# A two-layer streaming encoder on one core: masked attention over its decays, a fifth key tile, one inverse buffer, a split last norm, another seed

## The chip, the cores and the metric

The kernel runs on one core of one Trainium2 chip. The metric is the device time of one execution in microseconds, as the median over runs. The core has five engines that run side by side, each in the order in which its instructions are written: PE (matrix products, with its weight loads shown as PEld), DVE (vector work), ACT (scalar functions and copies), POOL (small vector work) and SP, which in this kernel issues all the DMAs. Semaphores hold an instruction back until what it reads is there.

## The reference

The input is x (2048 frames of 1024 values) with a conditioning vector c. There are two layers, each `x = x + gate * Mixer(RMSNorm(x) * (1 + scale) + shift)`, and a last RMSNorm. The first mixer is an RG-LRU block, the second a gated delta rule with 8 heads of width 128, in chunks of 64 in the reference:

```python
a_mat = where(strict, einsum(k_beta, k) * decay_mask, 0)
t_mat = triangular_solve(a_mat + eye, eye)
attn  = where(causal, einsum(q, k) * decay_mask, 0)
# step over the chunks:
v_new = u_c - w_c @ state
o_c   = q_c @ state + attn_c @ v_new
state = state * e_c + k_c.T @ v_new
...
y = rmsnorm(x, final_g)
```

All values are fp32.

## The kernel before

Frames are taken in two halves of 1024 (`u`), each in two pieces of 512 (`i`), each piece in four blocks of 128 (`b`). The projections are 512-wide products in which each fp32 factor is split in a high and a low part, three products for one (`products`, line 711). A weight panel of 1024x128 is loaded (`raw`), cast to its high part on ACT (`whi`) and, the first time, its low part is made on DVE (`wlo`).

In the second layer each head `h`, half `u` and piece `i` has threads of its own. `key_thread` loads the summed log decays as a row to all partitions (tile `ec`), masks them on POOL, takes the exponential on ACT, transposes the keys on PE (`pk`), copies them to `kd`, and multiplies the products of keys (`pkk`) by the decays to `ac`. `norm_q_thread` squares the queries reloaded in token order (`pq`), `value_thread` scales the values (`vn`). `query_thread` multiplies the products of keys and queries (`pqk`) by the decays to the masked attention `at` and then gives the decay tile back. `inverses_thread` inverts blocks of 32 on DVE, and `levels_thread` joins them to blocks of 128 with small products (`px`, `pr`) through the buffer `tf`. `recurrence_thread` then steps over the blocks: on PE `pp` (keys and queries with the state), on DVE `zt`, on PE `py`, on ACT `yt`, on PE `pS`, on DVE the new state. Each step waits for the one before, and projection products (`mm`) of later heads fill PE meanwhile. `t2` is ACT's scaled copy of the queries' product.

ACT holds one table of functions at a time: the exponential and the tanh need another than the silu that makes `kt`, `qt`, `vt` and the gate `tz`, and each change is an `ACT_TABLE_LOAD`.

The order on every engine is set before the kernel runs, by a planner (`Weave`): threads yield what they want next (an engine with a duration, a buffer, an event), and it always takes the one that can start first. The durations off PE are scattered by 1% with a random number from `SEED`, so another seed gives another order everywhere. Buffers are counted by `Slots`, a number for each tag: 3 for `ec`, 4 for `atn`, 4 for `kd`, 2 for `tf`. Tags in the pool `l2a` lie in a stretch of memory that is given back early, by `queries_end_thread`, to the rows and residuals of the last stage.

In the last stage (`out2_jobs`, products `mmo`) `final_thread` adds the residual and sums squares of each part of a block, and `finish_thread` normalizes it. The last block has three parts (512, 256, 256 columns).

Of the kernel before, what the change touches and what calls it, by code (L numbers as in the profile page):

```python
# [16 lines left out]
D = 1024  # L17
# [8 lines left out]
NH = 8  # L26
# [4 lines left out]
TURN = 2  # L31
BLK = 2
KTN, QTN = 6, 5
MARGIN = 1.0
EPS = 1e-6
SMALL = 161
# [1 line left out]

LAG = {"pe": 0.2, "act": 0.128, "dve": 0.113, "pool": 0.034}
WEIGHTS = 0.12  # L40
SEED, SPREAD = 3, 0.01
TABLE = 1.28
TRANSFER = {"sp": (1.56, 0.61, 0.05), "st": (0.74, 0.38, 0.5)}
SHARED = {"dve2": "pool2", "pool2": "dve2"}
# [126 lines left out]
def trunk_kernel(ctx, tc, x, head, small, ada0, ada_w, ada_b, final_g, w1, gate_w, ow1, w2, wab, ow2, out):  # L171
# [44 lines left out]
    def part_of(tile_in, at, *shape):  # L216
# [24 lines left out]
    tags |= {"edge1": ("l1", 1)}  # L241
    tags |= {"yf": ("o1", 1), "yh": ("o1", 2), "yl": ("o1", 2), "xr": ("o1", 2), "g1": ("o1", 1)}
    tags |= {t: ("l2", n) for t, n in {
        "xe": 2, "xf": 2, "kt": KTN, "qt": QTN, "vt": 1, "ec": 3, "gr": 1, "middle": 1, "ac": 4, "atn": 4, "kd": 4, "vn": 4,
        "rq": 4, "nk": 4, "oo": 2, "tblk": 1, "ttmp": 1, "tf": 2, "zt": 2, "t2": 2, "yt": 2, "so": 2, "ro": 2,
        "ssk": 2, "ssq": 2, "rk": 2, "cc": 2, "junk": 1, "ab": 1, "gin": 1, "gg": 1, "spe": 1, "spd": 1, "beta": 2,
        "gs": 2, "eg": 2}.items()}

    for t in ("xe", "xf", "vt", "ec", "gr", "middle", "ab", "gin", "gg", "spe", "spd"):
        tags[t] = ("l2a", tags[t][1])  # L250
    tags |= {"g2": ("o2a", 1), "fg": ("o2a", 1), "xta": ("o2a", 2)}
    tags |= {"oh": ("o2", 3), "ol": ("o2", 3), "xt": ("o2", 4), "ot": ("o2", 2)}
    slots = {t: Slots(n) for t, (_, n) in tags.items()}
    slots["turn"] = Slots(TURN)
    pools.update(xp=xp, ps=ps)
    phase, early = ExitStack(), ExitStack()

# [14 lines left out]
    def ev(*key):  # L272
        return events.setdefault(key, Event())

    def put(tag, token):
        w.put(slots[tag], token)
# [848 lines left out]
    def key_thread(u, h, i):  # L1125
# [2 lines left out]
        g_d = yield ev("grows", u)  # L1128
        etok = yield slots["ec"]
        yield "sp", 0.92  # L1130
        ec = tile_([P, TB, P], "ec", "ec")
        sp.dma_start(out=ec, in_=g_d[h:h + 1, i * TC:(i + 1) * TC].to_broadcast([P, TC]))
        yield "none", MARGIN / 2
        yield "pool", 0.779, MARGIN / 2
# [126 lines left out]
    def query_thread(u, h, i):  # L1261
        qt, qtok = yield ev("q", u, h, i)
        kt, ktok, ac, atok, ec, etok, kd, dtok = (yield ev("key", u, h, i))[:-2]
        ptok = yield slots["tp"]
        pqk = ps.tile([P, TB, P], F32, tag="tp", name="pqk")
        for b in range(TB):
            yield "pe", 0.224, 0.0
            pe.matmul(pqk[:, b, :], lhsT=kt[:, b * P:(b + 1) * P], rhs=qt[:, b * P:(b + 1) * P],  # L1268
                      start=True, stop=True)
        xtok = yield slots["atn"]  # L1270
        yield "dve", 0.61
        at = tile_([P, TB, P], "atn", "at")
        dve.tensor_tensor(at, pqk, ec, ALU.mult)
        put("tp", ptok)
        put("ec", etok)
        vn, ntk = yield ev("vn", u, h, i)
        toks = {"kt": ktok, "qt": qtok, "ac": atok, "atn": xtok, "kd": dtok, "vn": ntk}
        w.set(ev("parts", u, h, i), (kt, qt, ac, at, kd, vn, toks))

    def inverses_thread(u, h):  # L1280

# [114 lines left out]
    def recurrence_thread(u, h):  # L1396
# [4 lines left out]
        for i in range(NTC):  # L1401
# [7 lines left out]
            for b in range(TB):  # L1409
                m = i * TB + b  # L1410

                first, last = u + m == 0, u == NU - 1 and m == NB - 1
                kc, qc = kt[:, b * P:(b + 1) * P], qt[:, b * P:(b + 1) * P]
                if first:
                    pp = hold = None
                    zt = vn[:, b, :]
                else:
                    ptok = yield slots["d"]
                    yield "pe", 0.442
                    pp = ps.tile([P, 2, P], F32, tag="d", name="pp")  # L1420
                    pe.matmul(pp[:, 0, :], lhsT=kc, rhs=S_, start=True, stop=True)  # L1421
                    pe.matmul(pp[:, 1, :], lhsT=qc, rhs=S_, start=True, stop=True)  # L1422
                    hold = Hold(w, slots["d"], ptok, 2)
                if b == TB - 1:
                    release(toks, "kt", "qt")
                if not first:
                    ztok = yield slots["zt"]
                    yield "dve", 0.265
                    zt = tile_([P, P], "zt", "zt")
                    dve.scalar_tensor_tensor(zt, pp[:, 0, :], eg[:, 0, m, h:h + 1], vn[:, b, :], ALU.mult,  # L1430
                                             ALU.subtract)
                    hold.done()

                w.spawn(output_thread(u, h, m, pp, hold, oo[:, b, :], so[:, b:b + 1], eg), 1)
                ptok = yield slots["d"]
                yield "pe", 0.216
                py = ps.tile([P, P], F32, tag="d", name="py")
                pe.matmul(py, lhsT=rm[:, b, :], rhs=zt, start=True, stop=True)  # L1438
                if not first:
                    put("zt", ztok)  # L1440
                ytok = yield slots["yt"]
                yield "act", 0.18
                yt = tile_([P, P], "yt", "yt")
                act.activation(yt, py, AF.Copy, scale=1.0 if first else -1.0)
                put("d", ptok)
                ptok = yield slots["d"]
                yield "pe", M4 if last else 2 * M4
                pS = ps.tile([P, 2, P], F32, tag="d", name="pS")
                if not last:
                    pe.matmul(pS[:, 0, :], lhsT=kd[:, b, :], rhs=yt, start=True, stop=True)  # L1450
                pe.matmul(pS[:, 1, :], lhsT=at[:, b, :], rhs=yt, start=True, stop=True)  # L1451
                put("yt", ytok)
                hold = Hold(w, slots["d"], ptok, 1 if last else 2)
                w.set(ev("pS", u, h, m), (pS, hold))
                if b == TB - 1:
                    release(toks, "ac", "vn", "kd", "atn")
                if last:
                    return
                yield "dve", 0.258
                if first:  # L1460
                    dve.tensor_copy(out=S_, in_=pS[:, 0, :])
                else:
                    dve.scalar_tensor_tensor(S_, S_, eg[:, 1, m, h:h + 1], pS[:, 0, :], ALU.mult, ALU.add)
                hold.done()
# [73 lines left out]
    def queries_end_thread():  # L1538
        for i in range(NTC):
            yield ev("parts", NU - 1, NH - 1, i)  # L1540
            yield ev("rq", NU - 1, NH - 1, i)
        early.close()
        enter("o2a")
        w.set(ev("o2a"))
# [94 lines left out]
    def finish_thread(b, parts):  # L1639
        xt, tag, tok = yield ev("xt", b)  # L1640
        otag = "raw" if b < AHEAD else "ot"
        otok = yield slots[otag]
        stok = yield slots["ss"]
        ot = tile_([P, D], otag, "ot")
# [4 lines left out]
        if parts > 2:  # L1649
            yield "dve", 0.605  # L1650
            dve.tensor_tensor(xt[:, 0:TC], xt[:, 0:TC], fg[:, 0:TC], ALU.mult)
        for q in range(1, parts):
            yield ev("sq", b, q)
            yield "pool", 0.309
            pool.tensor_tensor(ss[:, 0:1], ss[:, 0:1], ss[:, q:q + 1], ALU.add)
        rtok = yield slots["rs"]
        yield "pool", 1.34
        rs = tile_([P, 1], "rs", "rs")
        rsqrt(rs, ss[:, 0:1], 1.0 / D, 1)
        put("ss", stok)  # L1660
        if parts > 2:
            yield "act", 0.628
# [133 lines left out]
```

## Time and profile before

| what | value |
|---|---|
| median of 3 runs | 1860.39 us (1857.08 to 1862.02) |
| the profiled execution, its own time | 1852.99 us |
| its span, first to last instruction | 1851.3 us |
| PE busy | 1798.8 us |
| ACT busy | 1167.0 us |
| granted clock, mean | 0.996 |

The span is what lies between the first and last instruction of one execution, and the time of that execution is 1.7 us more. A busy PE is a union of modelled intervals, so short gaps between products that overlap don't show in it. In the groups a line's idle time is that just ahead of its instructions, with what ended it.

### The profile page before, as it was taken

What the parts mean: (1) busy time and instruction counts of PE and PEld (TensorE: products, weight loads), DVE (VectorE), ACT (ScalarE), POOL (GpSimd) and SP (SyncE); (2) the same over time, 40 slices, a digit from 0 to 9 for tenths busy, and PEclk for the clock granted to TensorE, in tenths of its full rate; (3) what the DMA queues carried; (4) which work ended last, traced back from release to release, by engine and by line L of the source; (5) the groups of instructions that cost most, each with busy time, mean ns of one, the idle gap of its engine ahead of it and who ended that gap; (6) DMA issues with size and microseconds to landing.
All of it is one profiled execution on the core that took longest, in us unless ns stands there. A gap on an engine that the chain in (4) does not pass through costs nothing.

```text
span 1851.3 us, 31018 instructions
## 1 busy us (share of the span) xinstructions
PE 1798.8 (97%) x10270; PEld 1441.3 (78%) x10270; DVE 1344.0 (73%) x3112; ACT 1167.0 (63%) x2709; POOL 358.4 (19%) x896
## 2 busy tenths in 40 slices
PE   6999999999999999999999999999999999999998
PEld 4777777777878877787888787787788877778886
DVE  7989887877455647777888878577776687776653
ACT  5766777666111467786888766777778678654221
POOL 2111001010000013232323221232223223211100
PEclk9999999999999999999999999999999999999999
DMA  9577655545588645567677666366655556687741
GB/s 357 146 205 210 238 190 179 184 156 165 191 217 222 188 126 141 142 167 182 165 165 195 155 162 191 106 162 151 150 141 138 145 142 162 151 224 208 245 144 67
DMA packets 510425, 322.75 MB, mean 174 GB/s; under 512 B 369844, under 2 KB 437940, under 8 KB 510264
## 3 DMA queue, kind: packets, MB, share of 16 engines
q1 hardware_dynamic: 510264, 320.77, 62.0%
q8 instruction: 81, 1.33, 0.3%
q14 instruction: 80, 0.66, 0.1%
HBM read 219.93 MB, written 100.73 MB: 173 GB/s over the span
## 4 chain that ended last, share of the span: by engine, by line
PE 71%; DVE 9%; DMA 7%; ACT 7%; SPq 4%; issue 2%; POOL 1%; DVEq 0%; POOLq 0%; ACTq 0%
PE mm L711 39%; PE mmo L711 18%; PE pg L843 3%; DVE xf L763 2%; DMA raw<-in_w 2%; PE py L1438 1%; PE pp L1421 1%; PE pS L1450 1%; PE pS L1451 1%; PE pp L1422 1%; DVE ttmp L1303 1%; DVE tblk L1306 1%; DMA blk<-blk_d 1%; PE pqk L1268 1%; PE pkk L1180 1%
## 5 line engine op out<-in xcount | busy, mean ns | idle before, releaser
L763 DVE SCALAR_TENSOR_TENSOR xf<-xe,small_s,xf 128x512 f32<-128x512 f32 x288 | 214.1, 749 | 40.8 <-ACT xf L1021 37.2
L687 ACT CAST whi<-raw 128x1024 fp32r<-128x1024 f32 x96 | 100.0, 1042 | 50.1 <-DMA raw<-in_w 43.7
L1303 DVE TENSOR_TENSOR ttmp<-blk,tblk 128x60 f32<-128x60 f32 (+24 forms) x496 | 105.5, 213 | 17.3 <-DMA blk<-blk_d 5.7
L1306 DVE TENSOR_TENSOR tblk<-tblk,ttmp 128x60 f32<-128x60 f32 (+24 forms) x496 | 107.4, 217 | 12.2
L711 PE MATMUL mm<-hh_('in2', 0)_5148,whi 128*128 128x512 f32 x256 | 103.9, 406 | 2.2 <-DVE tf L1350 2.2
L711 PE MATMUL mm<-hh_('in2', 1)_11583,whi 128*128 128x512 f32 x256 | 104.5, 408 | 0.7 <-ACT tz L1036 0.7
L711 PE MATMUL mm<-hh_('in2', 0)_5148,wlo 128*128 128x512 f32 x256 | 104.2, 407 | 0.0
L711 PE MATMUL mm<-hh_('in2', 1)_11803,wlo 128*128 128x512 f32 x256 | 104.1, 407 | 0.0
L711 PE MATMUL mm<-hl_('in2', 1)_11584,whi 128*128 128x512 f32 x256 | 104.0, 406 | 0.0
L711 PE MATMUL mm<-hh_('in2', 1)_11583,wlo 128*128 128x512 f32 x256 | 104.0, 406 | 0.0
L711 PE MATMUL mm<-hl_('in2', 0)_5149,whi 128*128 128x512 f32 x256 | 103.8, 406 | 0.0
L711 PE MATMUL mm<-hl_('in2', 0)_5034,whi 128*128 128x512 f32 x256 | 103.6, 405 | 0.0
L711 PE MATMUL mm<-hl_('in2', 1)_11804,whi 128*128 128x512 f32 x256 | 103.5, 404 | 0.0
L711 PE MATMUL mm<-hh_('in2', 1)_11803,whi 128*128 128x512 f32 x256 | 103.5, 404 | 0.0
L711 PE MATMUL mm<-hh_('in2', 0)_5033,wlo 128*128 128x512 f32 x256 | 103.1, 403 | 0.0
L711 PE MATMUL mmo<-oh,oh 128*128 128x512 f32 (+1 forms) x264 | 102.8, 389 | 0.0
L711 PE MATMUL mmo<-ol,oh 128*128 128x512 f32 (+1 forms) x264 | 102.7, 389 | 0.0
L711 PE MATMUL mm<-hh_('in2', 0)_5033,whi 128*128 128x512 f32 x256 | 102.5, 400 | 0.0
L711 PE MATMUL mmo<-oh,ol 128*128 128x512 f32 (+1 forms) x264 | 102.4, 388 | 0.0
L711 PE MATMUL mmo<-oh,yl 128*128 128x512 f32 x256 | 100.5, 393 | 0.5 <-DVE yl L953 0.5
L711 PE MATMUL mmo<-oh,yh 128*128 128x512 f32 x256 | 100.8, 394 | 0.0
L711 PE MATMUL mmo<-ol,yh 128*128 128x512 f32 x256 | 100.8, 394 | 0.0
(317 smaller groups left out, 5322.0 us busy)
## 6 DMA issues: line engine op xcount, KB each, us to landing
raw<-in_w SPq DMA_DIRECT2D x96, 512.0 KB, 4.2
araw<-in_ada_w SPq DMA_DIRECT2D x32, 512.0 KB, 4.3
xt<-x_d SPq DMA_DIRECT2D x32, 512.0 KB, 5.4
xt_d<-xb SPq DMA_DIRECT2D x192, 64.0 KB, 2.7
xk<-xt_d SPq DMA_DIRECT2D x24, 512.0 KB, 5.7
xt<-in_x SPq DMA_DIRECT2D x16, 512.0 KB, 6.0
ada<-in_ada SPq DMA_DIRECT2D x16, 512.0 KB, 10.4
y_d<-tz SPq DMA_DIRECT2D x32, 256.0 KB, 3.0
```

The lines of the kernel that those rows point to most:

```text
L687: act.copy(hi, raw)
L711: pe.matmul(pt, lhsT=lhs[a][:, k, :], rhs=rhs[b][:, k, :], start=(k == 0 and n == 0), stop=(k == KT - 1 and n == 2))
L763: dve.scalar_tensor_tensor(xf, xe[:, 1 + j:1 + j + TC], wc[:, j:j + 1], xf, ALU.mult, ALU.add)
L843: pe.matmul(pg, lhsT=gw[:, g, :], rhs=xf, start=True, stop=True)
L1180: pe.matmul(pkk[:, b, :], lhsT=kc, rhs=kc, start=True, stop=True)
L1268: pe.matmul(pqk[:, b, :], lhsT=kt[:, b * P:(b + 1) * P], rhs=qt[:, b * P:(b + 1) * P], start=True, stop=True)
L1303: dve.tensor_tensor(tmp, blk[:, j, j + 1:32].unsqueeze(2).to_broadcast([P, r, c_]), t[:, j, 0:c_].unsqueeze(1).to_broadcast([P, r, c_]), A ...
L1306: dve.tensor_tensor(t[:, j + 1:32, 0:c_], t[:, j + 1:32, 0:c_], tmp, ALU.subtract)
L1421: pe.matmul(pp[:, 0, :], lhsT=kc, rhs=S_, start=True, stop=True)
L1422: pe.matmul(pp[:, 1, :], lhsT=qc, rhs=S_, start=True, stop=True)
L1438: pe.matmul(py, lhsT=rm[:, b, :], rhs=zt, start=True, stop=True)
L1450: pe.matmul(pS[:, 0, :], lhsT=kd[:, b, :], rhs=yt, start=True, stop=True)
```

## The change

Four things change, and the seed.

1. The masked attention is written over the decay tile: `query_thread` multiplies into `ec`, and the tag `atn` goes. The decay tile is given back at the end of its recurrence. Seven buffers (`EC`) are counted together, four of them in the pool `l2` and three, as `eca`, in the early stretch `l2a`; the counting is set so that the last uses fall on the four. `queries_end_thread` waits in addition until the last three that lie in the early stretch are free.
2. `kd` has five buffers instead of four, `tf` one instead of two.
3. For the last block the first two parts' sum is scaled and the epsilon added on POOL; when the last part's sum is there, one instruction on DVE adds it, scaled, and POOL takes the power. Before, POOL added the last part, scaled, and took the power.
4. `finish_thread` of the first eight blocks waits until all loads of the output weights are issued, before it takes one of the `raw` buffers.
5. `SEED` is 75 instead of 3.

```diff
--- before.py
+++ after.py
@@ -31,6 +31,7 @@
 TURN = 2
 BLK = 2
 KTN, QTN = 6, 5
+EC = 7
 MARGIN = 1.0
 EPS = 1e-6
 SMALL = 161
@@ -38,7 +39,7 @@
 
 LAG = {"pe": 0.2, "act": 0.128, "dve": 0.113, "pool": 0.034}
 WEIGHTS = 0.12
-SEED, SPREAD = 3, 0.01
+SEED, SPREAD = 75, 0.01
 TABLE = 1.28
 TRANSFER = {"sp": (1.56, 0.61, 0.05), "st": (0.74, 0.38, 0.5)}
 SHARED = {"dve2": "pool2", "pool2": "dve2"}
@@ -241,17 +242,19 @@
     tags |= {"edge1": ("l1", 1)}
     tags |= {"yf": ("o1", 1), "yh": ("o1", 2), "yl": ("o1", 2), "xr": ("o1", 2), "g1": ("o1", 1)}
     tags |= {t: ("l2", n) for t, n in {
-        "xe": 2, "xf": 2, "kt": KTN, "qt": QTN, "vt": 1, "ec": 3, "gr": 1, "middle": 1, "ac": 4, "atn": 4, "kd": 4, "vn": 4,
-        "rq": 4, "nk": 4, "oo": 2, "tblk": 1, "ttmp": 1, "tf": 2, "zt": 2, "t2": 2, "yt": 2, "so": 2, "ro": 2,
+        "xe": 2, "xf": 2, "kt": KTN, "qt": QTN, "vt": 1, "ec": 4, "eca": 3, "gr": 1, "middle": 1, "ac": 4, "kd": 5, "vn": 4,
+        "rq": 4, "nk": 4, "oo": 2, "tblk": 1, "ttmp": 1, "tf": 1, "zt": 2, "t2": 2, "yt": 2, "so": 2, "ro": 2,
         "ssk": 2, "ssq": 2, "rk": 2, "cc": 2, "junk": 1, "ab": 1, "gin": 1, "gg": 1, "spe": 1, "spd": 1, "beta": 2,
         "gs": 2, "eg": 2}.items()}
 
-    for t in ("xe", "xf", "vt", "ec", "gr", "middle", "ab", "gin", "gg", "spe", "spd"):
+    for t in ("xe", "xf", "vt", "eca", "gr", "middle", "ab", "gin", "gg", "spe", "spd"):
         tags[t] = ("l2a", tags[t][1])
     tags |= {"g2": ("o2a", 1), "fg": ("o2a", 1), "xta": ("o2a", 2)}
     tags |= {"oh": ("o2", 3), "ol": ("o2", 3), "xt": ("o2", 4), "ot": ("o2", 2)}
     slots = {t: Slots(n) for t, (_, n) in tags.items()}
+    ECLAST = NU * NH * NTC - 1
     slots["turn"] = Slots(TURN)
+    slots["ec"] = Slots(EC)
     pools.update(xp=xp, ps=ps)
     phase, early = ExitStack(), ExitStack()
 
@@ -1128,7 +1131,7 @@
         g_d = yield ev("grows", u)
         etok = yield slots["ec"]
         yield "sp", 0.92
-        ec = tile_([P, TB, P], "ec", "ec")
+        ec = tile_([P, TB, P], "eca" if (ECLAST - etok) % EC >= 4 else "ec", "ec")
         sp.dma_start(out=ec, in_=g_d[h:h + 1, i * TC:(i + 1) * TC].to_broadcast([P, TC]))
         yield "none", MARGIN / 2
         yield "pool", 0.779, MARGIN / 2
@@ -1267,15 +1270,12 @@
             yield "pe", 0.224, 0.0
             pe.matmul(pqk[:, b, :], lhsT=kt[:, b * P:(b + 1) * P], rhs=qt[:, b * P:(b + 1) * P],
                       start=True, stop=True)
-        xtok = yield slots["atn"]
         yield "dve", 0.61
-        at = tile_([P, TB, P], "atn", "at")
-        dve.tensor_tensor(at, pqk, ec, ALU.mult)
+        dve.tensor_tensor(ec, pqk, ec, ALU.mult)
         put("tp", ptok)
-        put("ec", etok)
         vn, ntk = yield ev("vn", u, h, i)
-        toks = {"kt": ktok, "qt": qtok, "ac": atok, "atn": xtok, "kd": dtok, "vn": ntk}
-        w.set(ev("parts", u, h, i), (kt, qt, ac, at, kd, vn, toks))
+        toks = {"kt": ktok, "qt": qtok, "ac": atok, "ec": etok, "kd": dtok, "vn": ntk}
+        w.set(ev("parts", u, h, i), (kt, qt, ac, ec, kd, vn, toks))
 
     def inverses_thread(u, h):
 
@@ -1453,7 +1453,8 @@
                 hold = Hold(w, slots["d"], ptok, 1 if last else 2)
                 w.set(ev("pS", u, h, m), (pS, hold))
                 if b == TB - 1:
-                    release(toks, "ac", "vn", "kd", "atn")
+                    release(toks, "ac", "vn", "kd", "ec")
+                    w.set(ev("ecfree", toks["ec"]))
                 if last:
                     return
                 yield "dve", 0.258
@@ -1539,6 +1540,8 @@
         for i in range(NTC):
             yield ev("parts", NU - 1, NH - 1, i)
             yield ev("rq", NU - 1, NH - 1, i)
+        for n in range(4, EC):
+            yield ev("ecfree", ECLAST - n)
         early.close()
         enter("o2a")
         w.set(ev("o2a"))
@@ -1639,6 +1642,8 @@
     def finish_thread(b, parts):
         xt, tag, tok = yield ev("xt", b)
         otag = "raw" if b < AHEAD else "ot"
+        if b < AHEAD:
+            yield ev("owissue", 2, 1)
         otok = yield slots[otag]
         stok = yield slots["ss"]
         ot = tile_([P, D], otag, "ot")
@@ -1649,14 +1654,23 @@
         if parts > 2:
             yield "dve", 0.605
             dve.tensor_tensor(xt[:, 0:TC], xt[:, 0:TC], fg[:, 0:TC], ALU.mult)
-        for q in range(1, parts):
+        for q in range(1, 2):
             yield ev("sq", b, q)
             yield "pool", 0.309
             pool.tensor_tensor(ss[:, 0:1], ss[:, 0:1], ss[:, q:q + 1], ALU.add)
         rtok = yield slots["rs"]
-        yield "pool", 1.34
         rs = tile_([P, 1], "rs", "rs")
-        rsqrt(rs, ss[:, 0:1], 1.0 / D, 1)
+        if parts > 2:
+            yield "pool", 0.28
+            pool.tensor_scalar(ss[:, 0:1], ss[:, 0:1], 1.0 / D, EPS, ALU.mult, ALU.add)
+            yield ev("sq", b, 2)
+            yield "dve", 0.16
+            dve.scalar_tensor_tensor(ss[:, 0:1], ss[:, 2:3], 1.0 / D, ss[:, 0:1], ALU.mult, ALU.add)
+            yield "pool", 0.6
+            pool.tensor_tensor(rs, ss[:, 0:1], mhalf[:, 0:1], ALU.pow)
+        else:
+            yield "pool", 1.34
+            rsqrt(rs, ss[:, 0:1], 1.0 / D, 1)
         put("ss", stok)
         if parts > 2:
             yield "act", 0.628
```

The order moves on all engines. Three places follow, the second of them on two engines, first as it stands before, then as it stands now. All names are those of the text above; `junkq` is the square of q's rows, `junk` that of the keys'.

ACT at the start of the second layer, before: what stands ahead of the fourth key tile (the last row).

```order
L1157 ACTIVATE junk,ssk<-kd 128x128 x2
L1021 ACTIVATE xf<-xe,small_s 128x512
L1219 ACTIVATE junkq,ssq<-pq 128x128 x3
L1139 ACT_TABLE_LOAD
L1139 ACTIVATE ec<-ec,gc 128x128
L687 CAST whi<-raw_5931 128x1024
L1139 ACTIVATE ec<-ec,gc 128x128 x6
L1219 ACTIVATE junkq,ssq<-pq 128x128
L1139 ACTIVATE ec<-ec,gc 128x128
L1028 ACT_TABLE_LOAD
L1028 ACTIVATE kt<-xf 128x512
```

ACT at the same place, now: the fourth key tile is the sixth row.

```order
L1160 ACTIVATE junk,ssk<-kd 128x128
L778 COPY xe<-mm 128x512
L1160 ACTIVATE junk,ssk<-kd 128x128 x2
L1024 ACTIVATE xf<-xe,small_s 128x512
L1160 ACTIVATE junk,ssk<-kd 128x128
L1031 ACTIVATE kt<-xf 128x512
L690 CAST whi<-raw_5934 128x1024
L1153 COPY kd<-pk 128x512
L1142 ACT_TABLE_LOAD
L1142 ACTIVATE ec<-ec,gc 128x128
```

The key tile has moved ahead of the squares of q, the decays, the panel cast and both table loads.

POOL at the end of the program, before.

```order
L1655 TENSOR_TENSOR ss_20002<-ss_20002 128x1
L281 TENSOR_SCALAR ss_20002<-ss_20002 128x1
L282 TENSOR_TENSOR rs<-ss_20002,mhalf 128x1
L1655 TENSOR_TENSOR ss_20066<-ss_20066 128x1 x2
L281 TENSOR_SCALAR ss_20066<-ss_20066 128x1
L282 TENSOR_TENSOR rs<-ss_20066,mhalf 128x1
```

POOL at the end of the program, now.

```order
L1660 TENSOR_TENSOR ss_19970<-ss_19970 128x1
L284 TENSOR_SCALAR ss_19970<-ss_19970 128x1
L285 TENSOR_TENSOR rs<-ss_19970,mhalf 128x1
L1660 TENSOR_TENSOR ss_20034<-ss_20034 128x1
L1665 TENSOR_SCALAR ss_20034<-ss_20034 128x1
L1670 TENSOR_TENSOR rs<-ss_20034,mhalf 128x1
```

DVE at the end of the program, now; its last-but-one row is the new instruction.

```order
L1635 TENSOR_TENSOR xt_19848<-mmo,xt_19848 128x256
L1633 TENSOR_TENSOR mmo<-mmo,g_18496 128x256
L1635 TENSOR_TENSOR xt_19848<-mmo,xt_19848 128x256
L1668 SCALAR_TENSOR_TENSOR ss_20034<-ss_20034 128x1
L1679 SCALAR_TENSOR_TENSOR ot<-xt_19848,rs,fg 128x512
```

One add has left POOL, and the scale stands on POOL ahead of the DVE instruction and the power behind it.

PE in the second head's inverse, before: from the first small products `px` to the next, `pr`.

```order
L1345 MATMUL px<-tf,ac 32x32 x16
L1450 MATMUL pS<-yt,kd 128x128
L1451 MATMUL pS<-yt,at 128x128
L711 MATMUL mm<-hl_('in2', 0)_5034,whi 128x512
L711 MATMUL mm<-hh_('in2', 0)_5033,wlo 128x512
L711 MATMUL mm<-hh_('in2', 0)_5033,whi 128x512
L1421 MATMUL pp<-state_99,kt 128x128
L1422 MATMUL pp<-state_99,qt 128x128
L711 MATMUL mm<-hl_('in2', 0)_5034,whi 128x512
L1357 MATMUL pr<-ac,tf 32x32 x2
L1359 MATMUL pr<-tf,ac 32x32
```

PE at the same place, now.

```order
L1345 MATMUL px<-tf,ac 32x32 x16
L1438 MATMUL py<-zt,ac 128x128
L714 MATMUL mm<-hh_('in2', 0)_5033,whi 128x512
L714 MATMUL mm<-hl_('in2', 0)_5034,whi 128x512
L714 MATMUL mm<-hh_('in2', 0)_5033,wlo 128x512
L714 MATMUL mm<-hh_('in2', 0)_5033,whi 128x512
L1450 MATMUL pS<-yt,kd 128x128
L1451 MATMUL pS<-yt,ec 128x128
L714 MATMUL mm<-hl_('in2', 0)_5034,whi 128x512
L714 MATMUL mm<-hh_('in2', 0)_5033,wlo 128x512
L1183 MATMUL pkk<-kt 128x128
L1421 MATMUL pp<-state_99,kt 128x128
```

Between `px` and `pr` stand two more steps of the recurrence and the second piece's `pkk` now; `pr` follows 34 rows behind `px`, not within these.

## The prediction

> **What bounds the kernel now.** I read the page's busy times and chain first, then the windows cut at the kernel's stages, then who PE waited for in the second layer.
>
> ```profile
> span 1851.3 us, 31018 instructions
> ...
> PE 1798.8 (97%) x10270; PEld 1441.3 (78%) x10270; DVE 1344.0 (73%) x3112; ACT 1167.0 (63%) x2709; POOL 358.4 (19%) x896
> ...
> PE 71%; DVE 9%; DMA 7%; ACT 7%; SPq 4%; issue 2%; POOL 1%; DVEq 0%; POOLq 0%; ACTq 0%
> ```
>
> PE is busy nearly all the time and carries most of the chain. Every engine runs its instructions in the written order, so PE loses time only where its next instruction is not ready. The windows say where (columns: stage, its length, then busy time and instructions of PE, PEld, DVE, ACT, POOL, the granted clock, the DMA share, GB/s):
>
> ```profile
> 0.00:56.00 56.00, 39.45 (x238) 27.97 (x238) 44.81 (x115) 30.05 (x51) 10.71 (x29) 0.97 0.76 296
> 56.00:452.00 396.00, 394.54 (x1621) 301.57 (x1621) 329.11 (x545) 276.66 (x375) 51.60 (x77) 1.00 0.61 190
> 452.00:630.00 178.00, 177.46 (x766) 143.44 (x765) 98.99 (x143) 43.48 (x54) 8.35 (x22) 1.00 0.75 217
> 630.00:1696.00 1066.00, 1039.75 (x6986) 846.77 (x6985) 788.97 (x2218) 781.13 (x2154) 271.53 (x722) 1.00 0.62 157
> 1696.00:1843.60 147.60, 147.57 (x665) 121.51 (x663) 80.48 (x93) 34.45 (x74) 15.29 (x43) 1.00 0.53 164
> ```
>
> The start (0 to 56 us) loses 56.0 - 39.5 = 16.5 us and is touched by nothing but the seed; I hold it fixed. The first layer and its output lose 2 us, the last stage nothing. The second layer, where all of the change but the last norm lies, loses 1066.0 - 1039.8 = 26.3 us. Its waits by releaser (columns: total us, times, longest):
>
> ```profile
> PE pk L1146 <- ACT kt L1028: 4.2, 4, 3.1
> PE pS L1450 <- ACT yt L1444: 3.8, 5, 1.4
> PE px L1345 <- DVE tf L1338: 2.5, 4, 1.2
> PE mm L711 <- DVE tf L1350: 2.2, 1, 2.2
> PE py L1438 <- DVE zt L1430: 1.9, 2, 1.4
> PE pqk L1268 <- ACT qt L1028: 1.8, 4, 0.7
> PE pp L1421 <- DVE state L1463: 1.8, 3, 0.8
> PE pr L1357 <- DVE tf L1350: 1.6, 2, 1.1
> ```
>
> ACT's three rows here are 9.8 us and DVE's five are 10.0; with the ten smaller rows of the same answer ACT has about 12 and DVE about 13. ACT is not full (781 of 1066 us), so it is late because of what stands ahead in its queue: table loads and work that waits for a DMA. The two largest ACT cases show both. The first is the wait of 3.1 us for the fourth key tile of the layer:
>
> ```profile
> 711.27 0.31 ACT L1219 ACTIVATE junkq<-pq 128x128 bf16<-128x128 f32 x1 [4.45 <-DMA pq<-q_d]
> ...
> 712.57 1.28 ACT L1139 ACT_TABLE_LOAD   x1
> ...
> 717.57 1.28 ACT L1028 ACT_TABLE_LOAD   x1
> 718.86 0.63 ACT L1028 ACTIVATE kt<-xf 128x512 f32<-128x512 f32 x1
> ```
>
> ACT stands 4.45 us for a DMA that the squares of q need, loads the table for exp, makes decays, loads the table for silu, and only then makes `kt`. The second is a step of the recurrence:
>
> ```profile
> 1507.83 1.05 ACT L687 CAST whi<-raw 128x1024 fp32r<-128x1024 f32 x1 [1.69 <-DMA raw<-in_w]
> ...
> 1509.54 1.28 ACT L1139 ACT_TABLE_LOAD   x1
> ...
> 1511.46 0.49 PE L1450 MATMUL pS<-yt,kd 128*128 128x128 f32 x2 [1.43 <-ACT yt L1444]
> ```
>
> A late weight panel and one table load stand ahead of `yt`, and PE waits 1.43 us.
>
> **The change part by part.** *Last norm.* The end of the chain before (start, length):
>
> ```profile
> 1844.86 0.20 ACT ot L1636
> ...
> 1845.18 0.19 POOL ss L1655
> ...
> 1845.46 0.19 POOL ss L281
> ...
> 1845.70 0.60 POOLq L1783
> ...
> 1846.32 0.75 DVE ot L1665
> ...
> L297 DVE SCALAR_TENSOR_TENSOR sp<-sp,sp_d 128x8 f32<-128x8 f32 x6 | 1.0, 167 | 0.2
> ```
>
> From the last sum of squares (1845.06) to the last multiply (1846.32) there are an add, a scale and a power on POOL, 1.26 us. After, the add and scale of the first two parts stand ahead of the last sum, under the last products, and one tiny DVE instruction and the power are left: 0.04 to reach DVE, 0.17 (L297, the nearest small one), about 0.12 to reach POOL (as 1845.06 to 1845.18), 0.60, 0.02: 0.95. Gain 0.3 us, between 0 (if the extra crossing of engines costs 0.3) and 0.55 (the add and the scale with their gaps, 1845.18 to 1845.70).
>
> *ACT's queue.* The new order has 40 table loads in the second layer where 62 stood. The profile's rows for all but two of the 62 are these:
>
> ```profile
> L1139 ACT ACT_TABLE_LOAD x29 | 37.2, 1283 | 0.5
> L1028 ACT ACT_TABLE_LOAD x23 | 29.5, 1283 | 0.4
> L1036 ACT ACT_TABLE_LOAD x8 | 10.3, 1283 | 1.1 <-PE mm L711 0.9
> ```
>
> 22 loads at 1.283 us are 28 us of ACT, nearly all of it beside PE's work: PE's waits for ACT are only 12 us, whatever their cause. The wait of 3.1 us has lost its cause, since in the new order the fourth `kt` stands ahead of the squares of q, the decays and both loads. I take it off whole (3.1). The other 9 us I cut in the proportion of the loads, 22/62: 3.2 us. Loads close to the recurrence fall further: 14 stood within two ACT instructions ahead of a `yt` or `t2`, now 5. Sum: 6.3 us. The ends are 0 (other instructions are late in their place) and 12 (no wait for ACT left); I take the middle, because one case is read from the order and the rest is a share.
>
> *PE's order.* A group of small products between the 512-wide ones costs a switch:
>
> ```profile
> 770.11 0.47 PE L711 MATMUL mm<-hh_('in2', 0)_5033,wlo 128*128 128x512 f32 x1
> 770.42 0.39 PE L711 MATMUL mm<-hh_('in2', 0)_5148,whi 128*128 128x512 f32 x1
> 770.65 0.40 PE L711 MATMUL mm<-hl_('in2', 0)_5149,whi 128*128 128x512 f32 x1
> ```
>
> The first wide product behind a group takes 0.31 us to the next, the second 0.23: 0.08 us a switch. The built program has 568 runs of wide products that end in something else, 561 before: +0.6 us, from 0 (beside a wait) to 0.6. Steps of the recurrence with fewer than three wide products to cover them are 18, 17 before: nothing. Between the first two products of the block inverses (`px`, `pr`) the work of PE is 3.8 us in the mean, 2.7 before, but three such stretches are 1.4 us or less, as before: I take DVE's 13 us as unchanged, with -4 to +4 for a new draw, the size of its two longest waits (2.2 and 1.4).
>
> *The shared tiles, the fifth key tile, one inverse block.* The mask product has the same shape and reads the same operands; only its output is the decay tile: 0. Seven tiles replace three and four. A decay tile is now held to the end of its recurrence, so the eighth load waits for the first recurrence; before, three loads waited for a mask product, and those for four recurrences: 3 + 4 = 7 as well. Still four `ac` and four `vn` let no more than four units run to the inverse, and the fifth `kd` only lets a transposition go earlier. With one `tf` for two, the decays of the second half and the inverses share a buffer; they meet twice. 0, from -2 to +3 (one more wait of the longest kind). The three tiles that lie where the last rows go must be free before these load: the load of `gate_d` stands earlier in SP's order, not later: 0. The last outputs now wait for the output weights' issue, which keeps `raw` buffers for the weights; the last stage has no idle time to win or lose: 0.
>
> The sum is -0.3 - 6.3 + 0.6 = -6.0 us. The profiled execution took 1852.99 us (its span 1851.3 and 1.7 around it), which would become 1847; it is faster than the median of the runs, 1860.39. From the median it gives 1854.4 us, 0.32% less. About 0.3%, 5.6 us, is what a measurement of this kernel can tell from no change.
>
> PE's busy row may hide room. PEld is busy 846.77 of 1066 us in the second layer (79%) and 121.51 of 147.6 in the last stage (82%), where PE never stops; at the last stage's density the second layer would take 1029 us, so up to 37 us could go where the busy row shows 26. [...]
>
> **The rivals.** *No change.* The order is new everywhere, so waits go and others come. For it: the groups behind the first key tiles, the number of wide products and thin covers are the same, and DVE's waits are half of the loss. Against: fewer loads in all and near the recurrence. Then -0.3 + 0.6 and a draw of some us: 1858 to 1862, at 1860.7.
>
> *Slower: late DMAs ahead of the recurrence.* ACT stands still for DMAs that PE's next step doesn't need.
>
> ```profile
> ACT whi L687 <- DMA raw<-in_w: 25.1, 16, 4.6
> ...
> pq<-q_d SPq DMA_DIRECT2D x32, 256.0 KB, 3.9
> ...
> DMA to landing us min/median/max: 8.3/8.3/8.3
> ```
>
> The load of `pq` that cost 4.45 us above landed after 8.3 us (last row) where the median of all is 3.9 (the row ahead). The new order has 110 of the scalings of `vn` and squares of `pq`, which wait for such loads, within five instructions ahead of a `yt` or `t2`; 87 stood there before. Panel casts there are 22 in both. One late load there costs PE the 4.45 us less the three wide products of cover (0.7): 3.7 us. Four more of them turn -6.0 into +8.8: 1869. Against it: this happened once in the layer with `pq`, and most waits for `raw` were covered. The change is slower from the fourth late one on.
>
> *The hidden room goes too.* If the smoother order wins half of the 26 us and a third of the 11 below them, -17 us: 1843. For it: fewer loads near the recurrence. Against: 0.08 us a switch makes most of those 11 us, and the switches stay.
>
> **How the numbers follow.** Forecast (1847 to 1857) 0.43, no change 0.33, late DMAs 0.14, hidden room 0.10. The forecast's cases lie on both sides of the bound: four in five of it and all of the hidden room are faster by over 0.3%, 0.44; the rest of it and the no-change cases within, 0.42; late DMAs slower, 0.14. The range reaches from the hidden room's end, 1843, to 1867, past the no-change cases to the point at which late DMAs decide (three of them: -6.0 + 11.1 = +5.1, 1865.5) and a us beyond.
>
> **What would show it.** Right: PE's wait for the layer's fourth `kt` is gone, 40 table loads in the second layer, PE's waits for ACT at 6 us, DVE's near 13, and from the last sum to the last multiply 0.95 us. The forecast is wrong if PE's idle time in the second layer stays at 26 us under other names, if ACT waits longer for `pq` or `vn`, or if the start moves.

## The result, and the profile after

The changed kernel took 1843.95 us (median of 4 runs, 1843.05 to 1846.1), the kernel before 1861.2 beside it (4 runs, 1857.08 to 1863.72): ratio 0.9911, 95% interval 0.9891 to 0.9932, or 17.25 us less. Measured again on another chip it took 1843.33 against 1856.51, ratio 0.9927 (0.9914 to 0.9941), 13.2 us less. The forecast was 1854.4 in a range of 1843 to 1867. The two profiled executions are only 9.9 us apart (1843.05 against 1852.99), so the traces can explain some 10 us. On the three chips of the experiments the kernel before had medians of 1855.5 to 1856.5; its first runs lay some 5 us above that.

The page of the changed kernel: span, busy times by engine, and the chain by engine.

```profile
span 1841.1 us, 30993 instructions
...
PE 1795.8 (98%) x10270; PEld 1440.4 (78%) x10270; DVE 1343.5 (73%) x3113; ACT 1136.6 (62%) x2683; POOL 359.1 (20%) x895
...
PE 66%; DVE 11%; DMA 9%; ACT 6%; SPq 4%; issue 4%; POOL 1%; DVEq 0%; POOLq 0%; ACTq 0%
```

ACT lost 30 us of work and the span 10.2. Where they went is read from windows cut at the same places in both kernels: at the first product of the second layer's gates (`pab`) and at the last `pS`. Columns are those of the prediction's windows. First the kernel before, then the changed one.

```profile
0.00:645.30 645.30, 626.75 (x2691) 485.55 (x2692) 483.15 (x819) 355.94 (x486) 71.21 (x132) 1.00 0.66 204
645.30:1695.40 1050.10, 1023.85 (x6914) 833.70 (x6913) 778.14 (x2198) 775.38 (x2147) 270.99 (x718) 1.00 0.62 158
1695.40:1851.30 155.90, 148.17 (x669) 122.02 (x667) 82.69 (x97) 35.68 (x77) 16.23 (x46) 0.99 0.51 160
```

```profile
0.00:646.50 646.50, 626.69 (x2690) 485.71 (x2691) 483.02 (x819) 350.62 (x482) 72.25 (x132) 1.00 0.66 204
646.50:1686.60 1040.10, 1021.35 (x6916) 833.01 (x6915) 778.51 (x2199) 750.51 (x2126) 270.86 (x718) 1.00 0.63 160
1686.60:1841.10 154.50, 147.73 (x667) 121.66 (x665) 81.98 (x96) 35.45 (x77) 16.04 (x45) 0.99 0.51 158
```

The part up to the second layer is 1.2 us longer, the end 1.4 shorter, and the second layer 10.0 us shorter. There PE's idle time fell from 26.25 to 18.75 us (length less PE busy), and PE's busy time fell by 2.5 us although it has the same products to make. PE's waits in the second layer after, by who ended them (total us, times, longest):

```profile
PE pr L1382 <- DVE tf L1376: 2.8, 5, 1.1
PE py L1438 <- DVE zt L1430: 2.7, 3, 1.6
PE px L1345 <- DVE tf L1338: 2.7, 6, 0.9
PE pqk L1271 <- ACT qt L1031: 2.5, 5, 1.0
PE mm L714 <- ACT tz L1039: 1.4, 2, 0.7
PE py L1438 <- ACT t L1478: 1.3, 2, 1.0
PE pk L1149 <- ACT kt L1031: 1.0, 2, 0.6
PE pgc L1101 <- DVE gg L1096: 1.0, 1, 1.0
PE pr L1357 <- ACT tf L1348: 1.0, 1, 1.0
PE pS L1450 <- ACT yt L1444: 0.8, 2, 0.5
PE pr L1357 <- DVE tf L1350: 0.5, 2, 0.3
```

The longest wait is 1.6 us where it was 3.1. ACT's rows are 8 us in sum (12 before), DVE's about 10 (13 before). The waits over 2 us are gone, 3.1 for ACT and 2.2 for DVE, and the many short ones are still there. The fourth `kt` of the layer shows the first of the two (the timeline after, with start, length, and idle time ahead):

```profile
710.36 0.63 ACT L1031 ACTIVATE kt<-xf 128x512 f32<-128x512 f32 x1 [2.10 <-DVE xf L766]
711.31 0.60 PE L1149 MATMUL pk<-ident,kt 128*128 128x128 f32 x4
712.55 1.28 ACT L1142 ACT_TABLE_LOAD   x1
```

ACT makes `kt` before the load, and `pk` has no bracket: PE did not wait.

The other 2.5 us fit the clock. Windows of 3.41 us in the kernel before, laid on one grid (PEclk is the number before the DMA share):

```profile
714.41:717.82 3.41, 2.08 (x10) 1.39 (x8) 2.61 (x9) 3.39 (x11) 0.39 (x2) 1.00 0.28 83
717.82:721.24 3.42, 1.70 (x10) 1.48 (x11) 2.97 (x14) 3.41 (x8) 1.57 (x5) 1.00 0.76 243
...
864.59:868.00 3.41, 1.64 (x23) 1.07 (x26) 2.32 (x4) 3.10 (x6) 1.22 (x5) 1.00 1.11 245
868.00:871.41 3.41, 3.41 (x55) 2.77 (x45) 3.35 (x8) 1.59 (x4) 1.00 (x5) 0.51 1.08 204
...
1042.09:1045.50 3.41, 2.26 (x38) 1.58 (x38) 2.42 (x6) 3.41 (x11) 0.34 (x2) 1.00 0.98 204
1045.50:1048.91 3.41, 3.41 (x58) 2.73 (x57) 2.89 (x5) 2.78 (x6) 1.50 (x7) 0.51 0.86 206
```

Twice PE ran a whole window at half clock, right after a window in which it had been busy for only 1.64 and 2.26 us. By its clock of 0.51 such a window does half the work and would cost an estimated 1.7 of its 3.41 us on top of the wait that came before it. Measured it is a little less: the run e3 below makes the same products in the same order and has full clock at both places, and there the kernel before takes 1.5 and 1.4 us longer (from a product just behind the wait to one near the window's end 5.20 us against 3.73, and 4.18 against 2.76). That is 2.9 us in the layer. The changed kernel has no such window in the second layer (clock 1.00 throughout). The wait of 3.1 us for the fourth `kt` was the longest of all but brought no half clock: it fell across two windows, which stayed busy for 2.08 and 1.70 us. In e3 the same wait is shorter, 2.4 us, but falls into one window, which is busy for 1.20 us, and half clock follows.

### The profile page after: what moved, and what is told of

Same layout as the page of the kernel before. It is cut to its first block, busy times and chain, and to the rows that moved or that the text cites. A ratio compares the mean times of both kernels' runs of the same rounds, so it can differ in the third digit from the quotient of the medians.

```text
span 1841.1 us, 30993 instructions
## 1 busy us (share of the span) xinstructions
PE 1795.8 (98%) x10270; PEld 1440.4 (78%) x10270; DVE 1343.5 (73%) x3113; ACT 1136.6 (62%) x2683; POOL 359.1 (20%) x895
## 4 chain that ended last, share of the span: by engine, by line
PE 66%; DVE 11%; DMA 9%; ACT 6%; SPq 4%; issue 4%; POOL 1%; DVEq 0%; POOLq 0%; ACTq 0%
PE mm L714 36%; PE mmo L714 17%; DMA raw<-in_w 4%; PE pg L846 3%; DVE xf L766 2%; DVE tblk L1306 1%; DVE ttmp L1303 1%; PE py L1438 1%; PE pp L1421 1%; PE pS L1451 1%; PE pS L1450 1%; PE pp L1422 1%; PE pqk L1271 1%; PE pkk L1183 1%; PE pab L1069 1%
## 5 line engine op out<-in xcount | busy, mean ns | idle before, releaser
L714 PE MATMUL mm<-hh_('in2', 1)_11607,whi 128*128 128x512 f32 x256 | 104.3, 407 | 0.7 <-ACT tz L1039 0.7
L714 PE MATMUL mm<-hh_('in2', 1)_11816,wlo 128*128 128x512 f32 x256 | 104.5, 408 | 0.0
L714 PE MATMUL mm<-hl_('in2', 1)_11608,whi 128*128 128x512 f32 x256 | 104.1, 407 | 0.0
L714 PE MATMUL mm<-hh_('in2', 1)_11816,whi 128*128 128x512 f32 x256 | 103.8, 405 | 0.0
L714 PE MATMUL mm<-hh_('in2', 1)_11607,wlo 128*128 128x512 f32 x256 | 103.5, 404 | 0.0
L714 PE MATMUL mm<-hl_('in2', 1)_11817,whi 128*128 128x512 f32 x256 | 103.3, 404 | 0.0
## 6 DMA issues: line engine op xcount, KB each, us to landing
ada<-in_ada SPq DMA_DIRECT2D x16, 512.0 KB, 10.2
```

The lines of the kernel that those rows point to most:

```text
L714: pe.matmul(pt, lhsT=lhs[a][:, k, :], rhs=rhs[b][:, k, :], start=(k == 0 and n == 0), stop=(k == KT - 1 and n == 2))
```

## The experiments

The theory after the result: the second layer is as long as PE's work plus PE's waits plus what half clock adds; the order on the engines decides the waits, and a table load counts only where it stands ahead of a late step. The rivals: the 22 table loads carry the gain; the new seed carries it; the key and inverse buffers carry it. Ratios are to the kernel before on the same chip, with the 95% interval. e1 to e4 ran on one chip, e5 to e8 on a second, e9 to e12 on a third.

**e1: the kernel before with the new seed.**

```diff
-SEED, SPREAD = 3, 0.01
+SEED, SPREAD = 75, 0.01
```

Expected: 

> The kernel before with the new seed alone. Its second layer has 68 table loads in the built order (62 with the old seed, 40 in the changed kernel). If the gain (17 us by the medians) comes with the shared decay tiles and their fewer table loads: within 6 us of the kernel before, 1855 to 1867. If it comes with the seed: 1844 to 1850.

1851.2 us against 1855.63, 0.9977 (0.9965 to 0.999). The seed by itself gives a quarter per cent, about a third of the whole, and it does so with 68 table loads in the second layer where the kernel before has 62.

**e2: the changed kernel with the old seed.**

```diff
-SEED, SPREAD = 75, 0.01
+SEED, SPREAD = 3, 0.01
```

Expected: 

> The changed kernel with the old seed. 36 table loads in the second layer. If the tiles and loads carry the gain: 1840 to 1850, and the first product py of the recurrence comes 3 to 6 us earlier than in the kernel before, as in the changed kernel. If the seed carries it: 1857 to 1864.

1859.22 us, 1.0019 (1.0009 to 1.0029): slower than the kernel before. The edits without their seed bring nothing here, though this kernel has 36 table loads in the second layer and the kernel before 62. PE waits for ACT twice for over 4 us there, and the timeline shows the wide products behind the first of these waits, and two shorter ones, at half clock:

```profile
1123.58 0.79 PE L714 MATMUL mm<-hh_('in2', 0)_5148,whi 128*128 128x512 f32 x1 [1.88 <-DVE tf L1376]
1124.17 0.63 PE L714 MATMUL mm<-hl_('in2', 0)_5149,whi 128*128 128x512 f32 x1
1124.60 0.63 PE L714 MATMUL mm<-hh_('in2', 0)_5148,wlo 128*128 128x512 f32 x1
1125.02 0.63 PE L714 MATMUL mm<-hh_('in2', 0)_5148,whi 128*128 128x512 f32 x1
```

The wide products start 0.43 us apart instead of 0.23. Half clock lasts 13.65 us here, four windows, of which PE was busy for 1.07, 1.12, 2.66 and 3.41 us; with 3.41 us at 986 and at 1307 the layer has 20.5 us at half clock, 15.1 of them busy.

**e3 and e4: one table for the second layer**, in the kernel before and in the changed one. Keys, queries, values and gate go through the tanh instead of the silu, in the same order, and so have other values. In the second layers of both kernels the changes between the exponential and the silu are the loads of 1.283 us (62 before, 40 after); the tanh had none after the silu: `beta`, a tanh at 657.89 in the kernel before, follows the silu of 647.00 with no load between.

```diff
-        act.activation(r, xf, AF.Silu)
+        act.activation(r, xf, AF.Tanh)
...
-        act.activation(tz, pt, AF.Silu)
+        act.activation(tz, pt, AF.Tanh)
```

Expected, before: 

> The kernel before in exactly its order, but the silu of the second layer is replaced by tanh (other values), which needs no table change, so that all 62 table loads of the second layer are gone and nothing else moves. If table loads carry PE's waits for ACT, as the forecast's largest term has it: 6 to 12 us less than the kernel before (its waits for ACT in the second layer are 12 us). If they only fill idle ACT time and late DMAs carry the waits: within 3 us.

Expected, changed: 

> The same replacement in the changed kernel, in exactly its order: 40 loads fewer. By the forecast's share (a table load costs PE about 0.1 to 0.2 us): 4 to 8 us under the changed kernel's 1844. If table loads are hidden: 1842 to 1846. If the gain of the change is that of its 22 fewer loads, this and the kernel before without loads come out at one time, within 3 us.

The kernel before without its 62 loads took 1848.51 us, 0.9963 (0.9951 to 0.9976): 6.9 us, or 0.11 us a load. The changed kernel without its 40 took 1837.0, 0.9898 (0.9882 to 0.9915); against its 0.9927 on another chip that is 0.29% or 5.4 us, 0.13 us a load, and against the 0.9911 of its first runs 2.4 us, 0.06 a load. A load of 1.283 us thus costs a tenth of its length or less, and 22 of them 1.3 to 3 us: less than a quarter of the 13.2. Windows of the second layer, first e3, then e4:

```profile
644.50:1693.00 1048.50, 1024.49 (x6914) 834.41 (x6913) 777.97 (x2198) 696.78 (x2085) 268.91 (x718) 1.00 0.62 158
```

```profile
644.80:1680.20 1035.40, 1018.73 (x6917) 833.68 (x6916) 778.08 (x2199) 699.39 (x2086) 270.62 (x718) 1.00 0.63 161
```

Both have the same work on ACT now, within 3 us, and the layers still differ by 13.1 us. The times, 1848.51 and 1837.0 on one chip, differ by 11.5. So the loads are not what parts the two kernels; PE idles 24.0 us in one and 16.7 in the other.

**e5 and e6: the changed kernel again, and with the old last norm.** The edit is that of e6.

```diff
-        for q in range(1, 2):
+        for q in range(1, parts):
...
+        rsqrt(rs, ss[:, 0:1], 1.0 / D, 1)
```

Expected, again: 

> The changed kernel once more, beside the others on one chip. From its first runs (0.9911 of the kernel before) 1839 where the kernel before takes 1855.6, at most 1843. The replacement of silu without a table change then gained 2 to 3 us there, at 1837.0; if it comes out at 1837 or less, the 40 loads cost nothing.

Expected, old norm: 

> The changed kernel in its order with the old last norm (POOL adds the last sum, scales, takes the power). The forecast's term says 0.3 us more than the changed kernel, at most 0.55; from the last product to the end 7.3 us where the changed kernel has 7.0. If the whole microsecond between the two traces' tails (8.0 and 7.0) is the norm's: 1 us more.

0.9927 (0.9914 to 0.9941) and 0.9917 (0.9904 to 0.9931): the time can't tell the norms apart. The traces can. The end of the changed kernel (first run), then of e6:

```profile
1835.62 0.19 ACT L1639 ACTIVATION_READ_ACCUMULATOR ot<-xt 128x1 f32 x1
1835.91 0.16 DVE L1668 SCALAR_TENSOR_TENSOR ss<-ss 128x1 f32<-128x1 f32 x1 [0.65 <-ACT ot L1639]
1836.16 0.55 POOL L1670 TENSOR_TENSOR rs<-ss,mhalf 128x1 f32<-128x1 f32 x1 [2.56 <-DVE ss L1668]
1836.74 0.75 DVE L1679 SCALAR_TENSOR_TENSOR ot<-xt,rs,fg 128x512 f32<-128x512 f32 x1 [0.67 <-POOL rs L1670]
```

```profile
1834.45 0.19 ACT L1639 ACTIVATION_READ_ACCUMULATOR ot<-xt 128x1 f32 x1
1834.78 0.19 POOL L1660 TENSOR_TENSOR ss<-ss 128x1 f32<-128x1 f32 x1 [2.62 <-ACT ot L1639]
1835.06 0.19 POOL L284 TENSOR_SCALAR ss<-ss 128x1 f32<-128x1 f32 x1
1835.34 0.55 POOL L285 TENSOR_TENSOR rs<-ss,mhalf 128x1 f32<-128x1 f32 x1
...
1835.92 0.75 DVE L1670 SCALAR_TENSOR_TENSOR ot<-xt,rs,fg 128x512 f32<-128x512 f32 x1 [1.82 <-POOL rs L285]
```

From the end of the last sum to the last multiply it is 0.93 us with the new norm (1835.81 to 1836.74) and 1.28 with the old (1834.64 to 1835.92). From PE's last product to the end the kernel before takes 7.71 us, e6 7.38 and the changed kernel 6.74; what of the whole microsecond is not the norm's lies behind the last multiply and was not followed up.

e5 shows more: one program, run twice, and one place. First e5, then the changed kernel's first trace (windows on the grid of each, and the PE row of the wait):

```profile
752.18:755.59 3.41, 2.01 (x22) 1.31 (x20) 3.28 (x9) 1.68 (x6) 0.00 (x0) 1.00 0.79 213
755.59:759.00 3.41, 3.41 (x12) 3.02 (x12) 2.56 (x12) 1.32 (x4) 0.00 (x0) 0.50 0.58 179
...
754.96 0.67 PE L1382 MATMUL pr<-ac,tf 64*64 64x64 f32 x14 [1.40 <-DVE tf L1376]
```

```profile
755.14:758.55 3.41, 3.24 (x30) 2.41 (x29) 3.18 (x12) 2.10 (x7) 0.00 (x0) 1.00 0.65 223
...
755.89 0.68 PE L1382 MATMUL pr<-ac,tf 64*64 64x64 f32 x14 [0.17 <-DVE tf L1376]
```

The same `pr` waited 1.40 us in one execution and 0.17 in the other, and the first paid a half-clock window for it. Executions of one kernel can differ by a wait and its window, 1.2 + 1.5 us here: from this `pr` to the `pS` behind the window it is 4.12 us in e5 (754.96 to 759.08) and 2.64 in the other (755.89 to 758.53). Not all of it lasts: at the end of the layer e5 is 1.7 us behind (1041.8 against 1040.1), because later waits are shorter in it.

**e7 and e8: a third seed**, in the kernel before and in the changed one (`SEED` 11 in both).

Expected, before: 

> The kernel before with a third seed, 72 table loads in the second layer. If the seed draws waits at random: anywhere within 8 us of the kernel before. If more loads are slower by 0.11 us each, as the kernel before without loads gave: 1 us slower.

Expected, changed: 

> The changed kernel with a third seed, 40 table loads. If the tiles and loads carry a gain of their own beside the seed's: less than the kernel before with the same seed by 3 us or more. If the order is a draw and the tiles are worth nothing: as likely slower as faster than that one; the old seed gave 3.6 us more with the tiles and the new one gave less.

1876.34 us, 1.0107 (1.0091 to 1.0122), and 1857.24, 1.0005 (0.9993 to 1.0017). e7 lies outside both of its expectations. Both lose 8 to 10 us ahead of the second layer, which the change does not touch. Between them the edits make 1.0% here, 0.5% at seed 75 (0.9927 by 0.9977), and cost 0.2% at seed 3: a tendency, from three draws, and no constant.

**e9 and e10: the parts apart, at seed 75.** e9 is the changed kernel with `"kd": 4` and `"tf": 2` as before, so the shared tiles without the other buffers (the new norm, which no time resolves, and the wait for the output weights stay in); e10 the kernel before with the new seed, `"kd": 5` and `"tf": 1`.

Expected, e9: 

> The changed kernel with four key tiles and two inverse buffers as before; the seven shared tiles, the norm and the new seed stay. 42 table loads in the second layer of the built order, 40 in the changed kernel. If the shared tiles carry what the change has beside the seed (0.9977 with the new seed alone, 0.992 with all): 0.990 to 0.995 of the kernel before. If the fifth key tile carries it: 0.996 to 1.000.

Expected, e10: 

> The kernel before with the new seed, five key tiles and one inverse buffer, but the decays and the masked attention apart (3 and 4). 78 table loads. If the shared tiles carry it: 0.996 to 1.001 of the kernel before, not under the seed alone (0.9977). If the fifth key tile carries it: 0.990 to 0.995.

1845.95 us, 0.9943 (0.9925 to 0.996), and 1872.95, 1.0089 (1.0067 to 1.0111). The shared tiles take e1's 0.9977 most of the way to 0.9927. The key and inverse buffers, which end that way by -0.16%, inside the noise, cost 1.1% when they are put on the kernel before, which lies outside both expectations. e10 is one draw of the order too, and draws of the kernel before alone differ by 1.3%, so the 1.1% can't be laid on the buffers. Second layer of e9, then of e10:

```profile
645.10:1687.40 1042.30, 1021.30 (x6903) 834.35 (x6902) 772.58 (x2195) 752.10 (x2127) 262.14 (x718) 1.00 0.62 159
```

```profile
644.60:1722.60 1078.00, 1042.43 (x6939) 847.04 (x6938) 781.50 (x2202) 797.46 (x2167) 272.67 (x718) 0.98 0.61 155
```

e10 idles 35.6 us on PE and has 34 us at half clock, 28 of them busy, so an estimated 14 us of work lost at most. Its built order has 78 table loads in the layer, e9's 42. In the built orders the loads by seed (3, 75, 11) are 62, 68, 72 before and 36, 40, 40 after; with the shared tiles alone 38, 42, 42. So the shared tiles cut the loads, and neither the seed nor the other buffers. Why they do is not shown.

**e11 and e12: no wait for `pq`.** The square of q's rows reads a constant tile, so it waits for no load and the norm of q has other values; e11 in the kernel before, e12 in e2.

```diff
-            act.activation(junk, pq[:, b, :], AF.Square, accum_out=ss[:, b:b + 1])
+            act.activation(junk, ones, AF.Square, accum_out=ss[:, b:b + 1])
```

Expected, before: 

> The kernel before in exactly its order, but the squares of q read a constant tile instead of the reloaded rows (other values), so that ACT doesn't wait for those loads; the loads stay. ACT waited 6.9 us for them there, 4.45 at the place where PE then waited 3.1. If late loads ahead of ACT's queue carry PE's waits: 3 to 6 us less. If the table loads alone did: within 1.5 us.

Expected, changed with the old seed: 

> The same in the changed kernel with the old seed, which was 1.0019 of the kernel before: ACT waited 8.7 us for these loads there, and one wait of 4.4 us stood ahead of a wait of PE of 4.2 us. If the rival of late loads tells why this draw is slow: 4 to 8 us less, 0.998 or below. If not: 1.001 to 1.003.

1853.12 us, 0.9984 (0.997 to 0.9998), 2 to 3 us less, at the lower edge of what was expected if late loads carry PE's waits; and 1858.87, 1.0016 (1.0005 to 1.0027), as e2. PE's wait for the fourth `kt`, 3.1 us in the kernel before, in e3 and then in e11:

```profile
PE pk L1146 <- ACT kt L1028: 2.4, 1, 2.4
```

```profile
PE pk L1146 <- ACT kt L1028: 1.5, 1, 1.5
```

Without the two table loads 2.4 us of it stay, without the wait for `pq` 1.5: the late transfer weighed more than the tables. In e12 the wait only moved. ACT's waits for DMAs in e2, then in e12:

```profile
ACT junkq L1222 <- DMA pq<-q_d: 8.7, 3, 4.4
ACT tz L1039 <- DMA z_d<-tz: 4.4, 1, 4.4
```

```profile
ACT tz L1039 <- DMA z_d<-tz: 8.9, 1, 8.9
```

The next instruction in ACT's queue that needed a DMA stood for both, and PE's `pr` waited 4.4 us behind it (4.2 in e2). So e12 does not tell whether late loads as such made e2 slow; taking one away leaves the queue at the next.

The lengths of the second layer put together (PE idle is length less PE busy; half clock is the sum of PEclk's drops to a half):

| kernel | second layer | PE idle | at half clock |
|---|---|---|---|
| e4, changed, one table | 1035.4 | 16.7 | 0 |
| changed | 1040.1 | 18.8 | 0 |
| e6, changed, old norm | 1040.2 | 18.9 | 0 |
| e5, changed again | 1041.8 | 20.0 | 3.4 |
| e9, changed, `kd` 4, `tf` 2 | 1042.3 | 21.0 | 10.2 |
| e1, before, seed 75 | 1046.6 | 21.7 | 13.7 |
| e8, changed, seed 11 | 1048.0 | 24.6 | 17.1 |
| e3, before, one table | 1048.5 | 24.0 | 6.8 |
| e11, before, no `pq` | 1049.7 | 23.9 | 10.2 |
| before | 1050.1 | 26.3 | 6.8 |
| e12, changed, seed 3, no `pq` | 1056.7 | 28.8 | 23.9 |
| e2, changed, seed 3 | 1057.1 | 29.8 | 20.5 |
| e7, before, seed 11 | 1065.7 | 34.9 | 20.5 |
| e10, before, `kd` 5, `tf` 1, seed 75 | 1078.0 | 35.6 | 34.1 |

The layer's length follows PE's idle time but for e8, e3 and e11, which lie within 1.7 us of each other, and the half clock grows with both, though not row by row. The windows hold 114 (e9) to 151 (e10) products of the last stage (`mmo`), which the planner mixes in, at 0.23 us each; lengths of different orders are therefore comparable to some us only. The changed kernel has 128 and the kernel before 126.

## Why the prediction was right or wrong

The sign was right, but the time, 1843.95, lies 10.4 us under the forecast, at the lower end of the range, at the price of the rival of hidden room.

- **Last norm, -0.3.** Right in the trace: 0.93 us where 0.95 was forecast and 1.28 with the old code. No time resolves it. (The upper bound of 0.55 is 0.52 by the rows it names.)
- **ACT's queue, -6.3.** The mechanism was half right and the size too large. The wait for the fourth `kt` went, 3.1 us, for the reason given. PE's waits for ACT fell by 4 us in all, to 8 instead of 6. The step that failed is the share of 22/62, which took 3.2 us off ACT's other waits: outside the rows of `kt` they fell from 8.0 to 7.4 us. The loads were priced as the cause of these waits, and e3 and e4 give 1.3 to 3 us for 22 loads, a sum in which what they did to the fourth `kt` is already held.
- **PE's order, +0.6.** Not seen: PE's busy time fell by 2.5 us. With the 2.9 us of half clock set apart it would have risen by 0.4, which is too little to tell the charge of 0.08 us for each of seven switches from nothing.
- **DVE's waits, unchanged, within 4.** They fell from 13 to 10 us, inside the bound, with the wait of 2.2 us for `tf` gone.
- **Shared tiles and buffers, 0.** Wrong for the tiles. By the built orders it is the shared tiles that cut the loads, so the loads and the tiles were one term and not two; the tiles make 0.34% at seed 75 (e9 against e1), one draw. The key and inverse buffers make -0.16% on top of them, some 3 us and inside the noise; the +1.1% of e10 is on the kernel before, which the forecast didn't price.
- **A term that was missing: the clock.** The stretches at half clock stand in the kernel before, 1.4 to 1.5 us each on top of a wait. The windows of the prediction show a granted clock of 1.00 for the second layer, a mean in which 6.8 us at half speed cannot be seen. With them gone a long wait less is worth more than its own length: the traces' 10.0 us of the second layer are 7.5 of idle time and 2.5 of busy time. The rival of hidden room reached the right time by luck. It was right that busy time hides room, and the 2.5 us lie within its third of 11; but it gave no cause like the clock, and in the traces idle time gave 7.5 us where it counted on 13. The density of weight loads only followed the length: PEld is 833.70 of 1050.1 us in one kernel and 833.01 of 1040.1 in the other, 79.4 and 80.1%. The windows ahead of the two at half clock were not idle throughout: PE was busy for 1.64 and 2.26 us of their 3.41, and the longest wait ahead of the first was 2.22 us (before 866.18).
- **The base.** The gain was taken from the median, 1860.39, though the trace it was worked out from took 1852.99. The pair of traces shows 9.9 of the 16.4 us from that median. Of the other 6.5 about 3 come from first runs of the kernel before that lay high: it has 1855.5 to 1856.5 on three other chips, and on one of these the change makes 13.2 us. The 3 us between 13.2 and 9.9 stay open. The granted clocks leave little of it to half clock: on the chip of the 13.2 us the median over all executions is 0.994 before and 0.9965 after, where the two profiled ones have 0.996 and 0.998. A difference of 0.0025 instead of 0.002 is an estimated 0.9 us of work, less than the 1.8 us that one step of their last digit stands for.
- **The rivals.** No change: PE's idle time did not stay at 26 us. Late DMAs: ACT's waits for loads did not grow in the changed kernel (46 us in all, 45 before). One of the signs that the prediction named did come, without harm to PE: ACT waits longer for `vn` (1.4 us before, 7.5 now), but less for `pq` (6.9 before, 5.7 now):

```profile
ACT whi L690 <- DMA raw<-in_w: 23.9, 15, 4.5
ACT vn L1260 <- DMA vn<-v_d: 7.5, 6, 3.6
ACT junkq L1222 <- DMA pq<-q_d: 5.7, 2, 3.4
```

What each edit is worth apart from the draw stays open. At three seeds the edits together give +0.2, -0.5 and -1.0%. The draw spreads the same code by 1.3% (0.9977 to 1.0107 for the kernel before), more than the whole gain.

## What to carry to other kernels

Where one engine is busy 98% of the time, sum its waits and look at the granted clock in windows of a few us right behind the long ones: a wait of 2.2 us cost 1.5 us more than its length, and the layer's mean clock of 1.00 hid it. Price an instruction that is off the path by taking it away, not by its share of the count: a table load of 1.28 us cost 0.06 to 0.13 here. Where a planner with random numbers sets the order, run each version with several seeds before crediting an edit, and set a profile against the median of many runs.

## What the runs showed of the hardware

- PE's clock fell to a half for 3.41 us or a multiple of it (6.8 us in e9, 13.65 in e2), on one grid through the whole run: the starts at 21.5, 868.0, 1045.5 and 1847.7 in the kernel before lie 248.0, 52.0 and 235.0 steps apart, those at 986.3, 1116.0 and 1307.1 in e2 38.0 and 56.0.
- In the second layers of the kernel before, e1, e2, e3, e5, e9 and e10 every first half-clock window followed one with PE busy 2.42 us or less (the most in e10, at 1686.1). The converse does not hold: in the kernel before, windows with 2.08 and 1.70 us (at 714.4 and 717.8), without small products, brought no half clock, while 2.26 us (at 1042.1), of which 1.1 were small products of 32x32, did. Leaving out the products of 32x32 and 64x64, PE was busy for 1.50 us ahead of half clock in e2 (at 982.9) and for 1.23 ahead of full clock in e3 (at 1658.5), a narrower overlap than 1.70 to 2.42. So small products seem, by these windows, to count for less; what decides exactly stays open.
- A half-clock window cost 1.4 to 1.5 us at the three places where the same products in the same order ran at full clock in another run (two in the kernel before against e3, one in e5 against the changed kernel). A window in which PE was busy throughout did not always end it: that of e9 at 984.6, busy for all of its 3.41 us, was followed by a second one.
- A wait taken out of ACT's queue came back at the next late transfer: in e2 ACT waited 4.4 us for the load of `pq` and 4.4 for the store to `z_d` behind it, in e12 8.9 for the store alone.
